# Weights times values of the prompt: three passes over halves in place of one full-precision product

## The chip, the cores and the metric

The kernel runs on one core of one Trainium2 chip. The metric is the device time in microseconds of one execution; the profile is of one execution and gives the start and the length of each instruction on TensorE (PE, with its weight loads as PEld), VectorE (DVE), ScalarE (ACT), GpSimd (POOL) and the DMA queue of SyncE (SP).

## What is computed

One step of a hybrid decoder layer: half a SwiGLU feed-forward, a mixer (differential attention beside a gated short convolution), half a second SwiGLU. 1040 prompt positions (16 meta tokens and 1024 real ones) and 64 sample positions (8 sequences of 8, each with 1024 cached positions) go through it. The change touches only the attention of the prompt:

```python
def diff_attend(q, k, v, q_pos, k_pos, lam):
    s = jnp.einsum('bqhcd,bkhcd->bhcqk', q.astype(jnp.float32), k.astype(jnp.float32)) * (HEAD_DIM ** -0.5)
    mask = k_pos[None, :] <= q_pos[:, None]
    s = jnp.where(mask, s, NEG_INF)
    p = jax.nn.softmax(s, axis=-1)
    a = p[:, :, 0] - lam * p[:, :, 1]
    return jnp.einsum('bhqk,bkhe->bqhe', a, v.astype(jnp.float32))
```

There are 4 heads, two softmax maps of 64 columns in each, and values of 128 columns. Everything is float32.

## The kernel before, in words

The program has three stages: the first feed-forward with the input projection, the attention (the stage of this change), and the output projection with the second feed-forward. In the first and the last, TensorE multiplies in three passes: each operand is split into a high half `hi` (ACT copies it, rounded to the type float32r) and a low half `lo` (DVE subtracts `hi` from the original), and the helper `three` (lines 168 to 171) issues high times high, high times low, low times high. Each of the three is one weight load and one product. A product of plain float32 operands stands in the trace as two weight loads and two products.

In the attention stage the prompt is done in 36 jobs: 4 heads times 9 blocks of queries, in the order 8, 6, 7, 4, 5, 2, 3, 0, 1 of `qi` (block 0 is the 16 meta tokens, block `qi` has 128 queries and sees `qi` blocks of 128 keys and a last one of 16). A job has three steps, and three jobs run staggered:

- `scores` (qk, line 929): scores of both maps, already in three passes; DVE takes them out of PSUM with mask and running maximum (line 939).
- `weights`: exponentials on ACT, then POOL and DVE form the difference of the two maps.
- `flip`: TensorE transposes the weights, up to four 128x128 blocks into the one PSUM bank `fl` (line 967); they are copied to SBUF into `at` by DVE or ACT in turn (lines 969 and 970); then, for each block of keys, a plain float32 product with the values adds to the bank `po` (line 982). Blocks are added up over `j`. Every second job ends with a norm over `po` (`sub_norm`, lines 901 to 906).

The values of a head come by DMA (`load_v`) into `vbuf`, two buffers deep. `at` is four buffers deep. Between the steps of the prompt stand the turns of the samples' attention (the bank `sa`, lines 1024, 1046, 1059, 1063, 1072), spread evenly over the jobs. A scheduler orders the instructions within each engine; each engine then works in that order. SP's queue issues the loads.

## Time and profile before

| what | us |
|---|---|
| median of 3 runs (2293.79 to 2299.85) | 2297.01 |
| time of the profiled execution | 2293.83 |
| span of its trace | 2292.1 |
| PE busy over the span | 2136.1 |
| DVE, ACT, POOL busy over the span | 1404.7, 929.5, 299.8 |

The span runs from the first to the last instruction; 1.7 us of the profiled time lie around it. Busy time of PE counts each product to the modelled end of its pipeline, so that products overlap; how fast PE goes is read from the distance between starts. [...]

### The profile page before, as it was taken

What the parts mean: (1) busy time and instruction counts of PE and PEld (TensorE: products, weight loads), DVE (VectorE), ACT (ScalarE), POOL (GpSimd) and SP (SyncE); (2) the same over time, 40 slices, a digit from 0 to 9 for tenths busy, and PEclk for the clock granted to TensorE, in tenths of its full rate; (3) what the DMA queues carried; (4) which work ended last, traced back from release to release, by engine and by line L of the source; (5) the groups of instructions that cost most, each with busy time, mean ns of one, the idle gap of its engine ahead of it and who ended that gap; (6) DMA issues with size and microseconds to landing.
All of it is one profiled execution on the core that took longest, in us unless ns stands there. A gap on an engine that the chain in (4) does not pass through costs nothing.

```text
span 2292.1 us, 41517 instructions
## 1 busy us (share of the span) xinstructions
PE 2136.1 (93%) x16126; PEld 2038.4 (89%) x16126; DVE 1404.7 (61%) x2973; ACT 929.5 (41%) x1960; POOL 299.8 (13%) x419
## 2 busy tenths in 40 slices
PE   6899999999999979999799978749999999999997
PEld 5799999999999959999667768739999999999997
DVE  5766556655567775466457656765665665645756
ACT  7433333334254442333235555553333333332522
POOL 0111111110000004443302110001111111100000
PEclk9899999999999989999789889879999999999998
DMA  7121222235444313321567332112122222543443
GB/s 276 55 81 67 81 81 68 81 116 197 130 144 142 131 51 120 124 86 60 191 206 274 125 137 102 67 35 78 67 81 81 68 80 81 175 144 127 141 148 98
DMA packets 115240, 263.48 MB, mean 115 GB/s; under 512 B 14514, under 2 KB 56114, under 8 KB 107602
## 3 DMA queue, kind: packets, MB, share of 16 engines
q1 hardware_dynamic: 109698, 244.92, 31.7%
q0 software_dynamic: 5344, 15.90, 1.9%
q8 instruction: 126, 2.06, 0.4%
q14 instruction: 72, 0.59, 0.1%
HBM read 206.47 MB, written 61.97 MB: 117 GB/s over the span
## 4 chain that ended last, share of the span: by engine, by line
PE 51%; issue 31%; DVE 7%; POOL 5%; DMA 3%; ACT 2%; SPq 1%; POOLq 0%; ACTq 0%; DVEq 0%
PE mm L169 13%; PE mm L170 13%; PE mm L171 13%; POOL u L440 3%; POOL n L440 3%; PE po L982 2%; PE mm L296 2%; PE qk L929 2%; DVE X L176 2%; PE fl L967 1%; PE sa L1059 1%; PE st L204 1%; PE sa L1024 1%; DVE Y L546 1%; DVE Y L543 1%
## 5 line engine op out<-in xcount | busy, mean ns | idle before, releaser
L169 PE MATMUL mm<-X,W 128*128 128x276 f32 x3868 | 1130.1, 292 | 27.8 <-ACT W L175 10.5
L170 PE MATMUL mm<-X,W 128*128 128x276 f32 x3868 | 1127.2, 291 | 2.8 <-DVE X L176 2.8
L171 PE MATMUL mm<-X,W 128*128 128x276 f32 x3868 | 1126.6, 291 | 1.9 <-DVE W L176 1.9
L169 PEld LDWEIGHTS mm<-X,W 128*128 128x128 f32 x3868 | 732.0, 189 | 31.0 <-ACT W L175 11.4
L170 PEld LDWEIGHTS mm<-X,W 128*128 128x128 f32 x3868 | 733.0, 190 | 4.3 <-DVE X L176 4.0
L171 PEld LDWEIGHTS mm<-X,W 128*128 128x128 f32 x3868 | 733.3, 190 | 3.2 <-DVE W L176 3.2
L176 DVE TENSOR_TENSOR W<-WR,W 128x512 fp32r<-128x512 f32 (+3 forms) x421 | 329.1, 793 | 116.4 <-ACT W L175 114.8
L175 ACT ACTIVATE W<-WR 128x512 fp32r<-128x512 f32 (+3 forms) x421 | 284.1, 689 | 249.6 <-PE mm L170 134.8
L420 ACT ACTIVATE n<-mm 128x276 f32<-128x276 f32 x210 | 84.2, 401 | 317.5 <-PE mm L171 299.0
L586 DVE TENSOR_TENSOR Y<-Y,mm 128x276 f32<-128x276 f32 x288 | 126.3, 439 | 128.1 <-PE mm L171 123.4
L440 POOL TENSOR_TENSOR u<-u,R 128x276 f32<-128x276 f32 x93 | 75.1, 807 | 493.2 <-ACT u L471 265.3
L440 POOL TENSOR_TENSOR n<-n,R 128x276 f32<-128x276 f32 x83 | 65.4, 787 | 547.2 <-ACT n L449 547.2
L170 PE MATMUL mm<-X 128*128 128x276 f32 x416 | 121.9, 293 | 2.7 <-DVE X L176 2.7
L169 PE MATMUL mm<-X 128*128 128x276 f32 x416 | 123.0, 296 | 1.5 <-ACT X L175 1.5
L423 DVE TENSOR_TENSOR n<-mm,n 128x276 f32<-128x276 f32 x105 | 46.8, 445 | 125.7 <-PE mm L171 113.9
L171 PE MATMUL mm<-X 128*128 128x276 f32 x416 | 121.4, 292 | 0.0
L221 ACT ACTIVATE sq<-Y 128x276 f32<-128x276 f32 x168 | 68.2, 428 | 86.4 <-DVE Y L586 58.7
L176 DVE TENSOR_TENSOR X<-X 128x552 fp32r<-128x552 f32 x104 | 75.5, 728 | 38.4 <-ACT X L175 37.9
L169 PE MATMUL mm<-X,X 128*128 128x276 f32 x320 | 93.9, 293 | 0.0
L170 PE MATMUL mm<-X,X 128*128 128x276 f32 x320 | 93.1, 291 | 0.0
L171 PE MATMUL mm<-X,X 128*128 128x276 f32 x320 | 93.1, 291 | 0.0
L929 PE MATMUL qk<-q,q 64*128 64x336 f32 (+10 forms) x360 | 69.9, 385 | 15.5 <-ACT q L175 11.1
(174 smaller groups left out, 2669.3 us busy)
## 6 DMA issues: line engine op xcount, KB each, us to landing
WR<-in_w_gu SPq DMA_DIRECT2D x43, 1024.0 KB, 4.8
WR<-in_w_dn SPq DMA_DIRECT2D x48, 640.0 KB, 3.9
X<-hid SPq DMA_DIRECT2D x88, 276.0 KB, 4.1
kp<-in_cache_k SPq DMA_DIRECT2D x64, 256.0 KB, 3.9
vp<-in_cache_v SPq DMA_DIRECT2D x64, 256.0 KB, 4.4
hid<-u SPq DMA_DIRECT2D x93, 138.0 KB, 1.8
hid<-n SPq DMA_DIRECT2D x83, 138.0 KB, 1.7
WR<-in_w_in SPq DMA_DIRECT2D x11, 1024.0 KB, 4.9
```

Source lines behind the costliest of these rows:

```text
L169: nc.tensor.matmul(ps, lh, rh, start=first, stop=False, **kw)
L170: nc.tensor.matmul(ps, lh, rl, start=False, stop=False, **kw)
L171: last_pe[0] = nc.tensor.matmul(ps, ll, rh, start=False, stop=last, **kw).ins
L175: tc.keep_in_program_order(act.activation(hi, raw, AF.Copy))
L176: on.tensor_tensor(lo, raw, f32(hi), op=ALU.subtract)
L221: act.activation(sq, src[:, s], AF.Square)
L296: last_pe[0] = nc.tensor.matmul(banks[n, g], w, lay["yv"][p][:, c, g * G:g * G + G], start=c == PAIR_K[0], stop=c == PAIR_K[-1]).ins
L420: act.activation(t, ps, AF.Copy)
L423: dve.tensor_tensor(self.n1, ps, self.n1, op=ALU.add)
L440: on.tensor_tensor(t, t, lay["R"][p][:, g * G:g * G + G], op=ALU.mult)
L586: dve.tensor_tensor(y, y, ps, op=ALU.add)
L929: last_pe[0] = nc.tensor.matmul(pw[m], a[r, q0:q0 + P], b[r, k0:k1], start=n == 0, stop=n == 2, tile_position=(m * DH, 0)).ins
```

## The change

The product of weights and values is made in three passes. The values get a second buffer for the high half, and a new function `split_v` splits them (for head 0 at the start of the stage, for each next head at the seventh job of the head before). `flip` no longer copies the transposed weights: for each piece of the bank `fl`, ACT copies the rounded high half out of PSUM, and then DVE subtracts it from the same piece of PSUM, which gives the low half. The four buffers of `at` become two pairs. The products go through `three`.

```diff
-    vs = ring("vs0", 1, 1152)
+    vs = ring("vs0", 1, 1152, F32R)
...
-    vbuf = [v.rearrange("p (j e) -> p j e", j=9) for v in vs + ring("vs1", 1, 1152)]
+    vbuf = [[v.rearrange("p (j e) -> p j e", j=9) for v in (lo, hi)]
+            for lo, hi in (vs + ring("vh0", 1, 1152, F32R), ring("vs1", 2, 1152, F32R))]
     pbuf = ring("p", 6, TP)
-    abuf = [a.rearrange("p (j q) -> p j q", j=9) for a in ring("at", 4, 1152)]
+    abuf = [[a.rearrange("p (j q) -> p j q", j=9) for a in ring(f"at{n}", 2, 1152, F32R)] for n in range(2)]
...
+    def split_v(h):
+        lo, hi = vbuf[h % 2]
+        halves(hi[:, 0:8, :], lo[:, 0:8, :], f32(lo[:, 0:8, :]), dve)
+        halves(hi[:N_META, 8, :], lo[:N_META, 8, :], f32(lo[:N_META, 8, :]), dve)
...
     for n in range(2):
         split_qk(0, n)
+    split_v(0)
...
-            at = of(abuf, "at")
+            lo, hi = of(abuf, "at")
...
-                copy = lambda dst, src: (dve.tensor_copy(dst, src) if (qi + j0 // 4) % 2
-                                         else act.activation(dst, src, AF.Copy))
                 n = len(js) - (js[-1] == qi)
+                parts = []
                 if n:
-                    copy(at[:, j0:j0 + n, :rows], ps[:, :n * P].rearrange("p (j q) -> p j q", q=P)[:, :, :rows])
+                    parts.append((ps[:, :n * P].rearrange("p (j q) -> p j q", q=P)[:, :, :rows], slice(0, P), slice(j0, j0 + n)))
                 if js[-1] == qi:
-                    copy(at[:N_META, qi, :rows], ps[:N_META, n * P:n * P + rows])
+                    parts.append((ps[:N_META, n * P:n * P + rows], slice(0, N_META), qi))
+                for src, r, j in parts:
+                    act.activation(hi[r, j, :rows], src, AF.Copy)
+                    dve.tensor_tensor(lo[r, j, :rows], src, f32(hi[r, j, :rows]), op=ALU.subtract)
...
             for j in range(qi + 1):
                 kr = N_META if j == qi else P
-                nc.tensor.matmul(po[:, off:off + rows], vt_[:kr, j, :], at[:kr, j, :rows], start=j == 0, stop=j == qi)
+                three(po[:, off:off + rows], vt_[1][:kr, j, :], vt_[0][:kr, j, :], hi[:kr, j, :rows], lo[:kr, j, :rows],
+                      j == 0, j == qi)
...
+            if step % 9 == 7:
+                split_v(nxt)
```

Ahead of the attention stage, and behind its last norm, each engine's order is unchanged. On TensorE, where head 0 flips its first job (block 8), before: `fl` are the transposes, `po` the products, `qk` scores of later jobs.

```order
L967 MATMUL fl_11659<-WR,p_11361 128x128 x4
L982 MATMUL po_11668<-at_11367,vs_777_11327 128x128 x4
L929 MATMUL qk_11873<-q_776_11326,q_775_11325 128x272
L929 MATMUL qk_11873<-q_774_11324,q_775_11325 128x272
L929 MATMUL qk_11873<-q_776_11326,q_773_11323 128x272
L929 MATMUL qk_12046<-q_776_11326,q_775_11325 128x320
```

The same place in the changed kernel; `at_820` holds high halves of the weights, `at_819` low ones, `vh_810` high halves of the values, `vs_777` low ones.

```order
L169 MATMUL po_11677<-at_820_11370,vh_810_11360 128x128
L975 MATMUL fl_11666<-WR,p_11363 128x128 x4
L170 MATMUL po_11677<-at_819_11369,vh_810_11360 128x128
L171 MATMUL po_11677<-at_820_11370,vs_777_11327 128x128
L169 MATMUL po_11677<-at_820_11370,vh_810_11360 128x128
L170 MATMUL po_11677<-at_819_11369,vh_810_11360 128x128
L171 MATMUL po_11677<-at_820_11370,vs_777_11327 128x128
L169 MATMUL po_11677<-at_820_11370,vh_810_11360 128x128
```

Four products have become twelve, and the second group of transposes now stands behind the first of the twelve. On DVE, at the start of the stage before, between the first score chunks of head 0 (`ISA` is the masked reduction of a chunk and the reading of its maximum):

```order
L939 ISA p_11362,mx_11588<-qk_11590,WR 128x336
L939 ISA mx_11588 128x1
L879 TENSOR_REDUCE ls<-t_11372 128x2
L939 ISA p_11361,mx_11588<-qk_11599,WR 128x352
L939 ISA mx_11588 128x1
```

And there in the changed kernel:

```order
L947 ISA p_11364,mx_11594<-qk_11596,WR 128x336
L947 ISA mx_11594 128x1
L887 TENSOR_REDUCE ls<-t_11374 128x2
L176 TENSOR_TENSOR vs_777_11327<-vs_777_11327,vh_810_11360 128x1024
L947 ISA p_11363,mx_11594<-qk_11605,WR 128x352
L947 ISA mx_11594 128x1
L176 TENSOR_TENSOR vs_777_11327<-vs_777_11327,vh_810_11360 16x128
```

The two subtractions of the first head's values stand between its score chunks. On DVE where the second job is flipped, before:

```order
L969 COPY at_11368<-fl_11838 128x256
L969 COPY at_11368<-fl_11838 16x128
L955 SCALAR_TENSOR_TENSOR p_11361<-p_11361,sm_12038,p_11362 128x528
L200 SCALAR_TENSOR_TENSOR t_11375<-po_11668,t_11375 128x128
L939 ISA p_11366,mx_12112<-qk_12114,WR 128x272
```

And in the changed kernel, where ACT has ahead of each of these subtractions a copy out of the same `fl`:

```order
L985 TENSOR_TENSOR at_821_11371<-fl_11859,at_822_11372 128x512
L963 SCALAR_TENSOR_TENSOR p_11363<-p_11363,sm_12101,p_11364 128x528
L947 ISA p_11368,mx_12187<-qk_12189,WR 128x272
L947 ISA mx_12187 128x1
L200 SCALAR_TENSOR_TENSOR t_11377<-po_11677,t_11377 128x128
```

A piece of 128x512, which only ACT handled in this job before, now passes through DVE as well.

## Rows read from the trace of the kernel before

**Rows 1.** The page: busy time of engines, and granted clock in 40 slices.

```profile
PE 2136.1 (93%) x16126; PEld 2038.4 (89%) x16126; DVE 1404.7 (61%) x2973; ACT 929.5 (41%) x1960; POOL 299.8 (13%) x419
...
PEclk9899999999999989999789889879999999999998
```

**Rows 2.** The chain of work from 1090 to 1380 us, shares by line.

```profile
by line: PE po L982 16.7%; PE qk L929 15.2%; PE fl L967 8.9%; PE sa L1059 7.2%; PE sa L1024 5.9%; PE mm L170 4.3%; PE mm L171 4.2%; PE mm L169 4.2%; SPq L992 3.7%; issue 3.1%; DMA q<-k_spill 3.1%; PE po L903 2.9%; PE sa L1046 2.7%; DMA kp<-
```

**Rows 3.** Stretches: from:to, length, busy us (instructions) by engine, PEclk, DMA share, GB/s.

```profile
1117.00:1347.00 230.00, 217.44 (x1782) 155.10 (x1782) 146.19 (x548) 111.39 (x291) 44.71 (x74) 0.89 0.55 183
...
1149.00:1160.00 11.00, 10.93 (x99) 7.82 (x99) 2.15 (x8) 0.64 (x2) 0.60 (x1) 0.54 0.73 226
1160.00:1167.00 7.00, 6.23 (x55) 5.05 (x48) 3.53 (x14) 4.98 (x9) 0.49 (x1) 0.99 0.63 190
1167.00:1174.00 7.00, 6.48 (x38) 2.44 (x38) 4.38 (x13) 3.03 (x11) 1.41 (x3) 0.52 0.16 46
1174.00:1259.00 85.00, 84.11 (x780) 58.60 (x778) 57.68 (x225) 44.70 (x116) 15.83 (x22) 1.00 0.77 261
1259.00:1262.00 3.00, 2.76 (x14) 2.54 (x14) 2.63 (x8) 0.95 (x4) 1.02 (x1) 0.50 0.68 251
1262.00:1303.00 41.00, 40.54 (x396) 29.56 (x395) 26.71 (x104) 21.57 (x59) 7.11 (x10) 0.99 0.43 138
1303.00:1314.00 11.00, 11.00 (x45) 5.95 (x44) 6.64 (x20) 6.38 (x14) 2.10 (x3) 0.53 0.33 110
1314.00:1320.00 6.00, 6.00 (x52) 5.20 (x49) 4.71 (x20) 2.77 (x8) 1.68 (x2) 1.00 0.01 3
1320.00:1324.00 4.00, 4.00 (x19) 3.00 (x18) 1.91 (x8) 2.03 (x7) 0.05 (x1) 0.57 0.00 0
```

**Rows 4.** PE's products of weights and values: ns min/median/max; eight at full, eight at half clock.

```profile
L982 PE MATMUL po<-at,vs x360: 257/275/579, 1137.1 to 1345.2; 128*128 128x128 f32 x144, 16*128 16x128 f32 x32, 16*128 16x16 f32 x4
...
1333.11 1.06 PE L982 MATMUL po<-at,vs 128*128 128x128 f32 x8
...
1260.15 1.91 PE L982 MATMUL po<-at,vs 128*128 128x128 f32 x8
```

**Rows 5.** Timeline, start and length in us: float32r loads, and plain products of 64 columns.

```profile
1335.36 0.41 PEld L929 LDWEIGHTS qk<-q,q 64*128 64x128 f32 x3 [0.17 <-DVE mx L939]
...
1202.38 2.14 PE L1046 MATMUL sa<-s_comb,s_p 128*128 128x64 f32 x18
```

**Rows 6.** Timeline of three passes with 276 columns, and their loads over the run (page).

```profile
1100.15 0.29 PE L171 MATMUL mm<-X,W 128*128 128x276 f32 x1
...
1100.27 0.29 PE L169 MATMUL mm<-X,W 128*128 128x276 f32 x1
...
1100.40 0.29 PE L170 MATMUL mm<-X,W 128*128 128x276 f32 x1
...
L169 PEld LDWEIGHTS mm<-X,W 128*128 128x128 f32 x3868 | 732.0, 189 | 31.0 <-ACT W L175 11.4
L170 PEld LDWEIGHTS mm<-X,W 128*128 128x128 f32 x3868 | 733.0, 190 | 4.3 <-DVE X L176 4.0
```

**Rows 7.** Lines, 1117 to 1347 us: count, busy us, mean ns, idle before and releasers.

```profile
L982 PE MATMUL po<-at,vs 128*128 128x128 f32 (+2 forms) x360 | 59.9, 298 | 1.1 <-DVE at L969 0.7 <-ACT at L970 0.4
L939 DVE CUSTOM_DVE_ANT_0 p<-qk,WR 128x336 f32<-128x336 f32 (+10 forms) x120 | 55.6, 480 | 41.4 <-PE fl L967 27.1 <-PE qk L929 13.6
...
L982 PEld LDWEIGHTS po<-at,vs 128*128 128x128 f32 (+1 forms) x360 | 48.6, 198 | 11.3 <-issue 3.7 <-DVE at L969 1.8 <-ACT at L970 0.7
...
L967 PE MATMUL fl<-WR,p 128*128 128x128 f32 (+2 forms) x180 | 34.2, 302 | 2.8 <-ACT at L970 1.9 <-DVE p L955 0.5 <-DVE at L969 0.3
...
L967 PEld LDWEIGHTS fl<-WR,p 128*128 128x128 f32 (+2 forms) x180 | 19.3, 140 | 13.6 <-ACT at L970 2.3 <-issue 2.2 <-DVE at L969 1.1
L969 DVE COPY at<-fl 16x128 f32<-16x128 f32 (+4 forms) x40 | 16.6, 439 | 4.9 <-PE fl L967 4.8
L970 ACT ACTIVATE at<-fl 16x128 f32<-16x128 f32 (+5 forms) x44 | 15.1, 371 | 30.8 <-PE fl L967 30.4
```

**Rows 8.** Lines by form: a split of 128x1024 elsewhere, on DVE and ACT.

```profile
L176 DVE TENSOR_TENSOR X<-WR,X 128x1024 fp32r<-128x1024 f32 x6 | 7.3, 1223 | 14.6 <-ACT X L175 14.6
...
L175 ACT ACTIVATE X<-WR 128x1024 fp32r<-128x1024 f32 x6 | 6.2, 1048 | 0.0
```

**Rows 9.** The start of the stage in the timeline: PE waits for DVE's score chunks.

```profile
1121.73 8.76 PE L929 MATMUL qk<-q,q 64*128 64x352 f32 x33 [1.65 <-DVE mx L939]
```

More of the change, by code (lines that the diff above doesn't have):

```diff
@@ L862, in load_v @@
     def load_v(h):
-        dma(vbuf[h % 2][:, 0:8, :], v_spill[h, :, 0:8, :])
-        dma(vbuf[h % 2][:N_META, 8, :], v_spill[h, :N_META, 8, :])
+        lo = f32(vbuf[h % 2][0])
+        dma(lo[:, 0:8, :], v_spill[h, :, 0:8, :])
+        dma(lo[:N_META, 8, :], v_spill[h, :N_META, 8, :])
+    def split_v(h):
+        lo, hi = vbuf[h % 2]
+        halves(hi[:, 0:8, :], lo[:, 0:8, :], f32(lo[:, 0:8, :]), dve)
+        halves(hi[:N_META, 8, :], lo[:N_META, 8, :], f32(lo[:N_META, 8, :]), dve)
     load_qk(0)
```

## The prediction

> **What bounds the kernel now.** I read the page first, then the chain of work around the attention, then that stage in stretches, then single rows of PE. PE is busy for 93% of the span, far ahead of DVE and ACT [rows 1]. The changed lines work from 1117 to 1347 us alone. There the chain runs mostly through PE: the products of weights and values (po) are its largest line, then the scores (qk) and the transposes (fl) [rows 2]. PE is busy for 217.4 of these 230 us, DVE for 146.2, ACT for 111.4 [rows 3]. So PE sets the pace, and only 12.6 us are free on it. The second thing to see is the clock: PEclk, close to 1 in the feed-forwards, dips in the slices of this stage [rows 1]. Cut by clock, the stage has 36 us at half clock between 1149 and 1324 (11, 7, 3, 11 and 4 us) [rows 3]. At full clock PE goes through 55 + 780 + 396 + 52 = 1283 instructions in 139 us, 9.2 in each us; at half clock through 99 + 38 + 14 + 45 + 19 = 215 in 36 us, 6.0 in each us, or 4.6 without the first stretch, which is full of small sample products. A us at half clock thus loses 1 - 6.0/9.2 = 0.35 to 1 - 4.6/9.2 = 0.50 us.
>
> **What one product costs.** There are 180 products of weights and values, which stand as 360 pairs of a weight load and a product [rows 4]. Eight of them take 1.06 us to the end of the last, whose own length is 0.275: their starts are (1.06 - 0.275)/7 = 0.112 us apart, so a plain product costs 2 x 0.112 = 0.224 us. At half clock eight take 1.91 us, about 0.22 apart. After the change the same product is three pairs. What does one pair with a 128-column stationary and 128 moving columns of float32r cost? No row has it, and two bounds stand around it. Below: the feed-forward's three passes start 0.125 us apart with 276 columns [rows 6], 0.45 ns a column, which for 128 columns would be 0.058 us if moving columns were all that counts. Above: the weight load. The loads of three float32r score products with only 144 columns start (0.41 - 0.19)/2 = 0.11 us apart (0.19 is the mean length of a load in [rows 6]). The plain products of line 1046 move half as many columns as those of line 982, and yet eighteen of them take 2.14 us, (2.14 - 0.275)/17 = 0.110 apart [rows 5]. Halving the columns saved nothing: with 128 stationary columns, the load sets the distance. I take 0.112 us. Nor is a load spared because the first two of the three passes share their stationary: the feed-forward has the same sharing, and both passes have 3868 loads [rows 6].
>
> [...]
>
> **The change, step by step.**
> 1. PE: 180 more pairs at 0.112 us are 20.2 us. At the present share of half clock, 36 of 175 us (20%), they cost a further 180 x 0.2 x (0.22 - 0.112) = 3.9 us. Sum 24 us. The 16-row blocks cost one more load like the others. PE is the busy engine and works in order, so I hide none of it; if all the idle 12.6 us took it up, 11 would stay.
> 2. ACT and DVE: 84 copies (40 on DVE, 44 on ACT, 31.7 us together [rows 7]) become 84 copies on ACT and, behind each, 84 subtractions on DVE. At the mean lengths of these rows that is 84 x 0.371 + 84 x 0.439 = 68 us: 16 us more on ACT, 20 more on DVE. Both stay under PE (127 and 166 of 230 us). What counts is that a group of transposes now passes two engines in a row before the bank `fl`, of which there is one, is free, and before the second of the three passes can start. Behind a waiting transpose on PE stand scores and sample products, and DVE in turn already waits 27.1 us for transposes at its score reductions [rows 7]. Before, PE stood idle for the copies for 1.9 + 0.3 + 0.7 + 0.4 = 3.3 us, and its loads for 5.9 us: 10 to 19% of the copies' 31.7 us. The same share of the added 36 us is 4 to 7 us; I take 5. Ends: 0, if the scheduler's other work between the groups covers it (the order shows scores put there), and all 36.
> 3. The values' split: 1.05 us on ACT and 1.22 on DVE [rows 8], and a small piece, four times. For head 0 it stands on DVE between the first score chunks, for which PE already waits 1.65 us [rows 9]; I add 1.5 us there. The other three lie in the middle of the stage under PE, at nothing: if that cover is gone, 4.5 us. The two new buffers only move addresses. `at` gets two buffers in place of four, which holds a flip back only if two jobs' products are outstanding; in the order a job's products stand close behind its flip. Nothing for that.
> 4. The clock. This is the term that no row prices. What PE did before its falls at 1259 and 1303 was scores, transposes and small sample products; plain po products belong to what it did in the long stretch at full clock. [...] I take the half clock to grow from 36 to about 100 us of a stage of some 270 us: 64 us more, at the middle price of 0.43, are 27.5 us. Ends: none more, 0; and all of the remaining full-clock work, 139 us plus the added 20, at half clock: 159 x (9.2/6.0 - 1) = 85 us.
>
> Sum: 24 + 5 + 1.5 + 27.5 = 58 us. The profiled execution took 2293.8 us, 3.2 under the median of the runs shown, so it would become 2351.8, and on the scale of the median 2355 us.
>
> **The rivals.**
> - *The clock holds* (slower, but by less). For it: PE will be as busy as before, and from 1174 to 1259 the clock stayed up through the same mixture. Against it: each fall came out of a mixture that was already near one. Steps 1 to 3 alone are 30 us: 2327 us; with the loads' part of step 2 covered, 2319.
> - *The clock stays down* for nearly all of the stage. [...] Against it: the sample products of line 1059 are spread over the whole stage, and after them the clock rose (1314). 30 + 85 = 115 us: 2412 us or over.
> - *Products cost what they stream* (faster). If a float32r load hides behind the product ahead of it better than these rows show, the pair costs the lower bound of 0.058 us: three are 0.174 against 0.224, 9 us less over 180 products. With 1.5 us for the split and the flips covered it ends at 2290 us; it decides from 0.072 us a pair, where the gain, 180 x (0.224 - 3 x 0.072) = 1.5 us, is no more than the split costs. [...] Against it stand the rows of lines 929 and 1046.
> - *The second load is spared.* The product then costs two loads, as now, and only steps 2 and 3 stay: 2297 to 2304 us. Against it: the equal counts of loads in the feed-forward.
>
> **How the numbers follow.** I give the forecast 0.55 (2333 to 2395), the clock that holds 0.26, the clock that stays down 0.12, products at the price of streaming 0.03, the spared load 0.04. What a measurement of this kernel can tell from no change is 0.3%, 6.9 us, so faster is under 2290 and slower over 2304. The streaming case lies on its lower edge and gives 0.02 to faster and 0.01 to no change; the spared load gives 0.03 to no change and 0.01 to slower; everything else is slower: 0.94. The range that leaves out 2 in 10 reaches from 2316, the low end of the holding clock, to 2400.
>
> **What would show it.** In the profile of the changed kernel: 540 products of weights and values with 540 loads, eight of them in a row at full clock still near 0.11 us apart (streaming case: near 0.06; spared load: a third fewer loads). The stage, 230 us before, at 255 to 265 (clock holds) or near 285, the rest of the span unchanged to a few us. Half-clock stretches that sum to some 100 us between the stage's first rise and its end. Idle of PE for the lines that split the weights under 15 us. I am wrong above all if the granted clock of the stage stays where it is, or if PE's waits for the splits, not its products, make up the growth.

## The result and the profile after

The changed kernel takes 2395.63 us (median of 4 runs, 2391.38 to 2403.27), the kernel before on the same chip 2295.40 (4 runs, 2288.08 to 2299.85). The ratio is 1.0444, interval [1.0402, 1.0485]: slower by some 100 us. The forecast was 2355, in a range of 2316 to 2400.

First the page of the changed kernel, the lines that answer to [rows 1].

```profile
PE 2224.4 (93%) x16306; PEld 2109.3 (88%) x16306; DVE 1430.6 (60%) x3025; ACT 949.1 (40%) x2008; POOL 296.5 (12%) x419
...
PEclk9899999999999989997778757888999999999998
```

There are 180 more instructions on PE and as many more loads, and ten slices in a row stand at 5 to 8 tenths of TensorE's full clock, where before the lowest was 7 and nines stood between. Next the stretches of the changed kernel, as in [rows 3]: from:to, length, then busy us (instructions) of PE, PEld, DVE, ACT and POOL, then PEclk (the share of the full clock that was granted, in the mean of the stretch), DMA share and GB/s. The first is the whole stage; the others are four stretches at one level of the clock each, and the two at its end. Behind the dots stands the last head of the kernel before.

```profile
1117.00:1455.00 338.00, 306.58 (x1967) 225.27 (x1967) 176.98 (x608) 138.56 (x348) 44.77 (x78) 0.70 0.41 133
1179.00:1200.00 21.00, 20.89 (x180) 14.64 (x173) 10.11 (x44) 8.87 (x28) 1.84 (x4) 0.99 0.65 207
1251.00:1275.00 24.00, 22.02 (x205) 17.05 (x202) 14.62 (x58) 12.35 (x35) 2.92 (x6) 0.99 0.67 225
1309.00:1336.00 27.00, 23.91 (x268) 16.45 (x267) 17.18 (x56) 13.54 (x34) 3.77 (x6) 1.00 0.50 164
1336.00:1360.00 24.00, 23.49 (x95) 16.57 (x95) 9.12 (x39) 7.70 (x24) 1.24 (x3) 0.50 0.06 16
1374.00:1439.00 65.00, 60.18 (x227) 49.33 (x226) 26.21 (x94) 24.05 (x69) 8.73 (x15) 0.50 0.03 11
1439.00:1462.00 23.00, 12.41 (x44) 10.00 (x44) 9.59 (x16) 9.57 (x19) 1.08 (x2) 0.50 0.68 253
...
1324.00:1348.00 24.00, 20.36 (x129) 15.29 (x127) 15.47 (x62) 14.21 (x45) 7.01 (x13) 0.99 0.13 42
```

The mean clock of the stage went from 0.89 [rows 3] to 0.70. At full clock PE still goes through (180 + 205 + 268)/72 = 9.1 instructions a us, at half clock through (95 + 227)/89 = 3.6 in these two stretches, the thinnest ones; over all stretches at half clock from 1152 to 1439 it is 778 in 163 us, 4.8. From 1374 on, through the rest of the last head, the clock does not come back at all. In the kernel before, the last head ran from 1324 to 1348 at 0.99.

From here on the stage is counted from its first score product to the first product of the output projection: 237.7 us before, 332.6 after. The rows of the stage counted so, before and after:

```profile
1117.30:1355.00 237.70, 217.42 (x1782) 155.08 (x1782) 148.10 (x553) 113.43 (x294) 45.50 (x76) 0.88 0.56 184
...
1119.50:1452.10 332.60, 304.56 (x1963) 224.11 (x1963) 173.09 (x605) 133.52 (x342) 42.79 (x76) 0.71 0.40 131
```

The rest of the span is 2054.3 and 2057.0 us, so 94.9 of the 97.5 us between the two traces lie in this stage. PE's idle time in it went from 20.3 to 28.0 us.

Now the products themselves, in the timeline of PE of the changed kernel: start, length, line. The first three and the 16-row pair stand at full clock, the last three at half.

```profile
1265.80 0.28 PE L169 MATMUL po<-at,vs 128*128 128x128 f32 x1
1265.91 0.27 PE L170 MATMUL po<-at,vs 128*128 128x128 f32 x1
1266.02 0.27 PE L171 MATMUL po<-at,vs 128*128 128x128 f32 x1
...
1267.40 0.27 PE L170 MATMUL po<-at,vs 16*128 16x128 f32 x1
1267.51 0.27 PE L171 MATMUL po<-at,vs 16*128 16x128 f32 x1
...
1425.09 0.41 PE L170 MATMUL po<-at,vs 128*128 128x128 f32 x1
1425.31 0.41 PE L171 MATMUL po<-at,vs 128*128 128x128 f32 x1
1425.52 0.41 PE L169 MATMUL po<-at,vs 128*128 128x128 f32 x1
```

The starts are 0.11 us apart at full clock and 0.215 at half, just as the plain pairs of [rows 4] were (0.112 and 0.22). The pairs of a block of 16 rows are as far apart as those of 128, 0.11 us, and their loads are as long: 249 ns in the mean against 252 in line 171. Three passes are thus 0.336 us where one plain product was 0.224.

Then the groups of the stage that answer to [rows 7]: busy us, mean ns, idle before and releasers.

```profile
L171 PE MATMUL po<-at,vs 128*128 128x128 f32 (+2 forms) x180 | 60.1, 334 | 0.0
...
L985 DVE TENSOR_TENSOR at<-fl,at 16x128 fp32r<-16x128 f32 (+5 forms) x84 | 35.8, 427 | 20.5 <-ACT at L984 20.0
...
L984 ACT ACTIVATE at<-fl 16x128 fp32r<-16x128 f32 (+5 forms) x84 | 32.2, 384 | 86.5 <-PE fl L975 69.4 <-DVE at L985 16.8
```

84 copies and 84 subtractions take 32.2 + 35.8 = 68.0 us, as forecast to the us. New are the two waits between them: DVE waits 20.0 us for ACT's high half, and ACT 16.8 us for DVE to give the bank `fl` free.

### The profile page after: what moved, and what is told of

It is laid out like the page before. It is cut to its first block, busy times and chain, and to the rows that moved or that the text cites. A ratio compares the mean times of both kernels' runs of the same rounds, so it can differ in the third digit from the quotient of the medians.

```text
span 2389.6 us, 41983 instructions
## 1 busy us (share of the span) xinstructions
PE 2224.4 (93%) x16306; PEld 2109.3 (88%) x16306; DVE 1430.6 (60%) x3025; ACT 949.1 (40%) x2008; POOL 296.5 (12%) x419
## 4 chain that ended last, share of the span: by engine, by line
PE 59%; issue 22%; DVE 8%; POOL 4%; DMA 4%; ACT 3%; SPq 1%; POOLq 0%; ACTq 0%; DVEq 0%
PE mm L169 16%; PE mm L170 16%; PE mm L171 16%; POOL u L440 2%; PE qk L937 2%; PE mm L296 2%; DVE X L176 2%; POOL n L440 2%; PE po L169 1%; PE po L170 1%; PE fl L975 1%; PE po L171 1%; PE sa L1070 1%; DMA hid<-u 1%; PE sa L1035 1%
## 5 line engine op out<-in xcount | busy, mean ns | idle before, releaser
L937 PE MATMUL qk<-q,q 64*128 64x272 f32 (+10 forms) x360 | 84.6, 423 | 18.1 <-ACT q L175 10.9
```

What stands on the lines that cost most here:

```text
L937: last_pe[0] = nc.tensor.matmul(pw[m], a[r, q0:q0 + P], b[r, k0:k1], start=n == 0, stop=n == 2, tile_position=(m * DH, 0)).ins
```

## The experiments

Every run is given as a ratio to the kernel before on its own chip (medians there 2293.45, 2295.17 and 2288.02 us for the three groups of runs). Of each profile I read the stage from first score to first product of the output projection, in a row of the same form as above. The half-clock time is the sum of the stretches of the stage whose granted clock is half; 2 x (1 - PEclk) x length gives it from the row to some 3 us.

**One part at a time.** Four kernels take the change apart. The first has the splits of the weights but no use for them: the product is the plain one, of the high half alone (the low half and the values' split leave the result).

```diff
-                three(po[:, off:off + rows], vt_[1][:kr, j, :], vt_[0][:kr, j, :], hi[:kr, j, :rows], lo[:kr, j, :rows],
-                      j == 0, j == qi)
+                nc.tensor.matmul(po[:, off:off + rows], f32(vt_[0][:kr, j, :]), f32(hi[:kr, j, :rows]), start=j == 0, stop=j == qi)
```

> The weights are split as in the changed kernel (84 copies on ACT, 84 subtractions on DVE out of the one bank), but the values are not, and the product is the plain one of before, of the high half alone, so the low half of the weights is left out of the result. TensorE's work is that of before, the chain behind each group of transposes that of the changed kernel. Theory (three loads per product and the half clock make the growth): 5 to 25 us over the kernel before, 2300 to 2320 us. Rival (the waits for the two-engine split make it): most of the 100 us, 2360 to 2395 us.

It took 2336.39 us, ratio 1.0180 [1.0150, 1.0211]: 43 us over, between the two forecasts and far more than the first. First its stage row, then its waits (us in all, times, the longest), then the wait for the score reductions in the kernel before.

```profile
1119.70:1400.20 280.50, 247.20 (x1782) 173.27 (x1782) 167.00 (x597) 128.66 (x334) 45.18 (x76) 0.81 0.48 156
```

```profile
PEld po L991 <- ACT at L983: 17.5, 26, 1.9
...
PEld qk L936 <- DVE mx L946: 16.4, 29, 2.2
...
PE po L991 <- ACT at L983: 10.4, 16, 1.7
...
PE qk L936 <- DVE mx L946: 7.4, 14, 1.8
```

```profile
PEld qk L929 <- DVE mx L939: 9.0, 16, 2.1
```

PE does the same 1782 instructions as before, though in another order (as in the change, a job's next transposes now stand behind products of its first group), and stands idle for 280.5 - 247.2 = 33.3 us (before 20.3). Loads wait 17.5 us for the high half, where they waited 0.7 for ACT's copy and 1.8 for DVE's [rows 7]. The other large wait is at the scores: loads wait 16.4 us for DVE's score reductions, 9.0 before. DVE, it seems, is held up at the subtraction and comes late to the next scores.

The clock fell here too: the half-clock time of the stage is 106 us against 57 before, with the same products. So the chain alone, without one pass more, brings 50 us more of half clock.

The second keeps three passes but has one copy for each piece, by ACT and DVE in turn as before; the low half is left out (the high half stands in for it).

```diff
-                    act.activation(hi[r, j, :rows], src, AF.Copy)
-                    dve.tensor_tensor(lo[r, j, :rows], src, f32(hi[r, j, :rows]), op=ALU.subtract)
+                    copy(hi[r, j, :rows], src)
...
-                three(po[:, off:off + rows], vt_[1][:kr, j, :], vt_[0][:kr, j, :], hi[:kr, j, :rows], lo[:kr, j, :rows],
+                three(po[:, off:off + rows], vt_[1][:kr, j, :], vt_[0][:kr, j, :], hi[:kr, j, :rows], hi[:kr, j, :rows],
```

> One copy out of the bank per piece, by ACT or DVE in turn as before, values split, three passes that all take the high half of the weights (the low half is left out of the result). TensorE's work is that of the changed kernel, the chain that of before. Theory: 60 to 90 us over the kernel before, 2355 to 2385 us, with the half clock filling most of the last head. Rival (waits): 0 to 25 us, 2295 to 2320 us.

2330.76 us, ratio 1.0144 [1.0098, 1.0190]: 37 us over, between the two forecasts. Its stage row:

```profile
1120.20:1399.50 279.30, 261.73 (x1962) 199.78 (x1962) 153.68 (x560) 117.83 (x302) 44.38 (x76) 0.77 0.47 157
```

The third has one copy and two passes (low and high half of the values times the high half of the weights): as many loads and products as the kernel before, 360, but of float32r.

```diff
...
+                for n, v in enumerate((vt_[1], vt_[0])):
+                    nc.tensor.matmul(po[:, off:off + rows], v[:kr, j, :], hi[:kr, j, :rows], start=j == 0 and n == 0,
+                                     stop=j == qi and n == 1)
```

> As the run with three passes and one copy, but only two passes: high and low half of the values times the high half of the weights. [...] Theory (the thinner products themselves take the clock down): 25 to 60 us over the kernel before, 2320 to 2355 us, with more half clock in the stage. Rival (only the number of loads counts, and the clock follows the waits): within 10 us of the kernel before, 2287 to 2305 us.

2312.52 us, ratio 1.0092 [1.0059, 1.0125]: 19 us over, again between the two forecasts. Its stage row, and three of its passes in a row:

```profile
1120.50:1375.70 255.20, 234.76 (x1783) 170.29 (x1783) 153.28 (x561) 118.08 (x302) 44.41 (x76) 0.78 0.51 172
...
1183.14 0.27 PE L994 MATMUL po<-at,vh 128*128 128x128 f32 x1
1183.25 0.27 PE L994 MATMUL po<-at,vs 128*128 128x128 f32 x1
1183.36 0.28 PE L994 MATMUL po<-at,vh 128*128 128x128 f32 x1
```

Same count of pairs, same copies, nearly the same order on PE, the same 0.11 us between starts, PE's idle time as before (20.4 us against 20.3), and yet the half-clock time is 112 us against 57. What differs for PE is the kind of product: a float32r pass of 128 columns behind each load, where the plain product was. The values' split is in this kernel too, so that 17.5 us of stage are the price of both. Between the second and the third lie 180 pairs: 24.1 us of stage, with 17 us more of half clock.

One thing more lies between them. The function `three` also marks its last product as the one behind which the next turn of the samples is queued on TensorE (lines 171 and 1109); the plain product did not. This is in the change and in every run that calls `three`, and no run takes it out alone.

The chain alone (the first kernel) lengthens the stage by 42.8 us and the passes with the values' split (the second) by 41.7, each with the half clock that it brings. Together that is 84.5 of the 94.9 us; by ratio it is 74 of 102, and the rest needs both at once, or is noise.

The fourth adds work to the changed kernel that nobody reads: after the last turn of the samples, one float32r product of 512 columns for each key block, into an unread bank.

```diff
+                if not turns:
+                    nc.tensor.matmul(bank("sa"), vt_[1][:, 0, :], kh[:, :512], start=True, stop=True)
```

> The changed kernel, and once the samples are done one product more per block of keys: float32r, 128 rows, 512 moving columns, into a bank that nobody reads; about 30 products of 0.23 us at full clock, 7 us of added work. Theory (the clock of the last head is lost for want of dense work): 10 to 35 us under the changed kernel, 2360 to 2385 us, with full clock back between the end of the samples and the end of the stage. Rival (loads and waits, the clock is only a symptom): 5 to 10 us over the changed kernel, 2400 to 2406 us.

2408.41 us, ratio 1.0500 [1.0468, 1.0533]. The forecast missed: the 29 products did not bring the clock back, which stood at half for 1380 to 1435 and 1441 to 1475 us. Wide passes of this kind and number did not do it here. Four of them in a row, at half clock:

```profile
1421.81 2.07 PE L993 MATMUL sa<-q,vs 128*128 128x512 f32 x4
```

The median length is 0.735 us, so they start (2.07 - 0.735)/3 = 0.44 us apart; at full clock that would be some 0.22, an estimate from the 0.11 and 0.215 us of the narrow passes above, near the 0.23 of the forecast (512 columns at the 0.45 ns of [rows 6], an estimate as well).

**The clock.** So another sort was tried: the same added product, but of plain float32.

```diff
+                if not turns:
+                    nc.tensor.matmul(bank("sa"), f32(vt_[1][:, 0, :]), f32(kh[:, :512]), start=True, stop=True)
```

> The changed kernel with work added that nobody reads: once the samples' work is used up, one plain float32 product of 512 columns per key block into an unread bank, some 29 of them, about 25 us at the full clock (0.85 each) and up to 50 at half. Theory A, the half clock of the last head comes from thin products that leave the array idle while weights load, and a product that is wide and goes through more than one pass brings the clock back: half-clock time in the last head falls from 89 us to under 40, and the time is within 10 us of the changed kernel (2385 to 2405). Theory B, the clock is set by something else there: the half-clock stretch stays, and the time is 30 to 50 us over the changed kernel (2425 to 2445).

2403.31 us, ratio 1.0480 [1.0457, 1.0504], 8 us over the changed kernel by ratio, with intervals that overlap, though the 29 products add about 25 us of work: they are 58 pairs with a median length of 0.593 us, and four of these in a row start (1.88 - 0.593)/3 = 0.43 us apart. These four, then the stretches from the last samples to the projection in this kernel:

```profile
1412.92 1.88 PE L993 MATMUL sa<-q,vs 128*128 128x512 f32 x4
1414.73 0.50 PE L937 MATMUL qk<-q,q 64*128 64x16 f32 x3
...
1377.00:1404.00 27.00, 27.00 (x77) 18.00 (x77) 9.20 (x28) 6.21 (x16) 4.20 (x7) 0.50 0.03 8
1404.00:1452.00 48.00, 46.40 (x220) 29.33 (x218) 18.73 (x67) 17.60 (x53) 4.41 (x9) 1.00 0.06 18
```

In the middle of the last head the clock comes back from 0.50 to 1.00 and stays for 48 us, where the changed kernel had half clock throughout. What the first theory forecast came: with other work beside the same passes the clock was back. The reason that it gives, what the array does while weights load, was not shown. Nor is it shown whether it was the kind of work or its amount: 58 pairs at 0.43 us are 25 us, 29 float32r passes at the estimated 0.22 us are 6, so that this run added four times the work of the one before.

The other question on the clock is whether PE's idle time sets it. In the kernel before, PE is busy for 0.2 of the 11 us before the first scores (1106 to 1117) and for 0.4 of the 9 us before the output projection (1346 to 1355), and the clock stands at 0.50 behind both (1117 to 1121, 1355 to 1362). So products of constants were put into these two gaps of the kernel before (helper `warm`, 45 and 38 plain products of 128 columns, unread).

```diff
+    def warm(tag, n, after):
+        ps = bank(tag)
+        with tc.issue_after(after):
+            for _ in range(n):
+                nc.tensor.matmul(ps[:, :P], onesD, onesD, start=True, stop=True)
...
+    warm("sa", 45, last_pe[0])
...
+    warm("st", 38, norm_pe[0])
```

> The kernel before, with products of constants that nobody reads put where PE idles ahead of a fall of the clock: 45 plain 128 by 128 products ahead of the first scores of the attention stage (PE idle there for 11 us, and half clock right behind it) and 38 ahead of the output projection (9 us idle). Theory A, the clock falls there for the idle time, and these products keep it up: the half-clock stretch at the start of the stage goes, and the time is 4 to 12 us under the kernel before (2281 to 2289). Theory B, the fall comes from the thin products that follow, or the added products delay the first scores by as much as they save: within 4 us, or up to 8 us over.

2295.02 us (12 runs), ratio 0.9998 [0.9982, 1.0015]: no change, as the second theory had it. Its stretches at the start of the stage:

```profile
1106.00:1122.00 16.00, 15.07 (x130) 14.88 (x128) 2.72 (x5) 1.98 (x2) 4.91 (x8) 1.00 0.57 184
1122.00:1138.00 16.00, 14.78 (x106) 11.16 (x110) 12.56 (x43) 5.24 (x11) 6.20 (x18) 0.57 0.61 187
```

The clock stands at 1.00 through the gap, and falls to 0.57 all the same with the first scores. The half clock of the stage is 31 us against 57 and the stage 6.9 us shorter, but the first scores start 4.9 us later and the part behind the stage is 4.4 us longer. So the half clock at these waits cost little here, and what took it away cost as much.

**The split chain.** If the waits are for DVE's subtraction, the products with the low half could go last in each job:

```diff
...
+            for a, vs_ in ((hi, (1, 0)), (lo, (1,))):
+                for j in range(qi + 1):
+                    kr = N_META if j == qi else P
+                    for v in vs_:
+                        last_pe[0] = nc.tensor.matmul(po[:, off:off + rows], vt_[v][:kr, j, :], a[:kr, j, :rows],
+                                                      start=a is hi and j == 0 and v == 1, stop=a is lo and j == qi).ins
```

> The changed kernel with the order of the products within a job turned round: for each piece of weights first the two products that take the high half (low values times high, high values times high) for all key blocks, and the products that take the low half at the end. The same 540 load and product pairs, the same splits. Theory A, the waits of the split chain are for VectorE's subtraction, the later of the two reads: PE's waits at the products on VectorE (5.6 us in the changed kernel) go, the bank of the transposes is still held as long, so 5 to 15 us under the changed kernel (2380 to 2391). Theory B, what costs is the hold of the one transpose bank and the clock, not which half is ready first: within 4 us of the changed kernel (2391 to 2400).

2426.61 us, ratio 1.0573 [1.0550, 1.0595]: 30 us over the changed kernel, outside both forecasts. Its stage row and its waits, and after them the wait for ACT of the changed kernel:

```profile
1118.90:1482.40 363.50, 339.71 (x1962) 250.30 (x1962) 175.71 (x604) 135.24 (x342) 44.19 (x76) 0.62 0.37 120
```

```profile
PEld po L994 <- ACT at L984: 15.6, 22, 1.3
...
PE po L994 <- ACT at L984: 8.2, 15, 0.9
```

```profile
PEld po L169 <- ACT at L984: 6.5, 11, 1.3
```

The wait for DVE is gone, as meant, but the loads now wait 15.6 us for ACT (6.5 in the changed kernel): with the low products away, PE seems to reach the second piece of a job sooner, when its high half is not there yet. And the half clock grew from 196 to 275 us. That this follows from the order of the same 540 pairs is shown; why the clock took it so badly is not.

The other way is to free the bank after one read: a raw copy out of PSUM as before, and the split from that copy in SBUF, high half by ACT, low half by POOL.

```diff
...
+                    copy(raw[r, j, :rows], src)
+                    act.activation(hi[r, j, :rows], raw[r, j, :rows], AF.Copy)
+                    gp.tensor_tensor(lo[r, j, :rows], raw[r, j, :rows], f32(hi[r, j, :rows]), op=ALU.subtract)
```

> The changed kernel with one copy out of PSUM for each piece, by ScalarE and VectorE in turn as in the kernel before, and the split made from that copy in SBUF: the high half by ScalarE, the low half by GpSimd. The transpose bank is free after one read again, and VectorE has 84 subtractions fewer and half of the copies. Theory A, the hold of the bank over two engines and VectorE's load (about 25 us by the runs with an unchanged product) are what the split chain costs: 10 to 30 us under the changed kernel (2365 to 2386). Theory B, it is the length of the chain up to the first product that costs: here it is longer by a third operation, so the same or up to 30 us over it (2395 to 2425).

2364.72 us, ratio 1.0299 [1.0277, 1.0322]: 33 us under the changed kernel by ratio. The stage row, then the groups of the split, and the difference of the two maps on DVE in this kernel and in the changed one:

```profile
1121.70:1424.60 302.90, 283.95 (x1962) 212.92 (x1962) 173.84 (x560) 147.79 (x386) 112.19 (x160) 0.74 0.44 144
```

```profile
L990 POOL TENSOR_TENSOR at<-ar,at 16x128 fp32r<-16x128 f32 (+5 forms) x84 | 66.6, 805 | 98.5 <-ACT at L989 76.2 <-PE sa L1062 8.1 <-issue 6.2
...
L977 PE MATMUL fl<-WR,p 128*128 128x128 f32 (+2 forms) x180 | 39.8, 340 | 0.6 <-ACT ar L986 0.6
...
L964 DVE SCALAR_TENSOR_TENSOR p<-p,sm,p 128x1040 f32<-128x1040 f32 (+8 forms) x36 | 40.3, 1121 | 6.6 <-POOL p L963 6.6
...
L963 DVE SCALAR_TENSOR_TENSOR p<-p,sm,p 128x1040 f32<-128x1040 f32 (+8 forms) x36 | 27.4, 761 | 12.3 <-POOL p L962 12.3
```

POOL's subtraction takes 805 ns in the mean, DVE's took 427, and the chain is an operation longer: had its length been the cost, this would have been slower. It is faster, and what the edit freed is the bank, after one read. DVE's part of the copies shrank, but its busy time in the stage did not (173.8 us against 173.1 in the changed kernel): while POOL was busy for 112 us in place of 43, DVE's 36 differences of the two maps, unchanged in form, took 1121 ns in the mean in place of 761. PE's idle time is 18.9 us, less than before the change.

**Fewer loads.** The last four do the products of two neighbouring query blocks together. In the second job of a pair, key blocks that both read in full are multiplied once with 256 columns of weights: 396 pairs in place of 540.

```diff
...
-    abuf = [[a.rearrange("p (j q) -> p j q", j=9) for a in ring(f"at{n}", 2, 1152, F32R)] for n in range(2)]
+    lo2, hi2 = [a.rearrange("p (j s q) -> p j s q", j=9, s=2) for a in ring("at", 2, 2304, F32R)]
...
+            wide = qi - 1 if qi in (3, 5, 7) else 0
+            for j in range(wide):
+                three(po[:, :2 * P], vt_[1][:, j, :], vt_[0][:, j, :], hi2[:, j], lo2[:, j], j == 0, False)
+            for q, o in ((qi - 1, 0), (qi, P)) if wide else () if qi in (2, 4, 6) else ((qi, off),):
+                for j in range(wide, q + 1):
...
```

> The changed kernel with the products of two neighbouring query blocks done together, in the second job of each pair: for the key blocks that both read in full, each of the three passes moves 256 columns of weights past one load of values. 396 load and product pairs in place of 540 (144 of them 256 columns wide), the same splits, the weights of a pair in one tile. Theory A, the half clock comes from passes so thin that the load of the values takes as long as the product: 144 pairs fewer are 14 us, half-clock time in the stage falls by 40 us or more from 196, some 15 to 20 us, and part of the chain's 25 us is covered because the first block of a pair is long ready: 30 to 60 us under the changed kernel (2335 to 2365). Theory B, the clock follows the waits and not the width: only the pairs are saved, 10 to 18 us under it (2377 to 2386).

2354.99 us, ratio 1.0294 [1.0271, 1.0318]: 34 us under the changed kernel by ratio. The stage row, one job's wide passes, and the group that waits:

```profile
1117.10:1412.40 295.30, 259.13 (x1819) 187.22 (x1819) 171.44 (x605) 133.63 (x342) 43.98 (x76) 0.75 0.45 148
```

```profile
1161.52 0.28 PE L171 MATMUL po<-at,vs 128*128 128x256 f32 x1
1161.65 0.28 PE L169 MATMUL po<-at,vh 128*128 128x256 f32 x1
1161.76 0.28 PE L170 MATMUL po<-at,vh 128*128 128x256 f32 x1
1161.88 0.28 PE L171 MATMUL po<-at,vs 128*128 128x256 f32 x1
```

```profile
L975 PE MATMUL fl<-WR,p 128*128 128x128 f32 (+2 forms) x180 | 40.1, 344 | 10.7 <-DVE at L985 10.1 <-DVE nm L955 0.3 <-DVE nm L1052 0.2
```

Passes of twice the columns start 0.12 us apart in place of 0.11: the second 128 columns cost 0.01 us. Half clock is 145 us, 51 less than in the changed kernel. PE's idle time however is 36.2 us: without products between, the transposes now run into the bank that DVE's subtraction still holds (10.1 us).

The same kernel with every product at 128 columns holds back the first block's products but saves no load. Against the paired kernel:

```diff
-            wide = qi - 1 if qi in (3, 5, 7) else 0
...
-            for q, o in ((qi - 1, 0), (qi, P)) if wide else () if qi in (2, 4, 6) else ((qi, off),):
-                for j in range(wide, q + 1):
...
+            for q, o in ((qi - 1, 0), (qi, P)) if qi in (3, 5, 7) else () if qi in (2, 4, 6) else ((qi, off),):
+                for j in range(q + 1):
...
```

> The kernel with paired products, but every product 128 columns wide: 540 pairs as in the changed kernel, those of the first query block of a pair held back to the job of the second. Only the cover of the split chain differs from the changed kernel. Theory A, the chain of ScalarE, VectorE and product is what PE waits for in the changed kernel: half of the jobs no longer wait, 8 to 20 us under it (2375 to 2388). Theory B, the held products are a longer run of thin passes, with more half clock: as the changed kernel or up to 20 us over it (2395 to 2415).

2380.76 us, ratio 1.0413 [1.0390, 1.0437]: some 7 us under the changed kernel, with an interval that overlaps its own. Half clock is 191 us, as there. So of the pairing's gain most comes with the width.

Both helps together, the split from SBUF and the paired products, with both diffs:

> Both changes that should help the changed kernel: one copy out of PSUM for each piece with the split made from it in SBUF by ScalarE and GpSimd, and the products of two neighbouring query blocks done together at 256 columns. Theory A, the gains add, since one frees the bank and VectorE and the other cuts pairs and half clock: 31 us of the first and 30 to 60 of the second, 60 to 90 under the changed kernel (2305 to 2335), still over the kernel before. Theory B, both cover the same wait: no more than 10 us under the better of the two (2330 to 2365).

2337.31 us, ratio 1.0212 [1.0196, 1.0227]. That is 53 us under the changed kernel by ratio, where the two gains add up to 67: they add for the most part. The time lies just over the first forecast and in the range of the second, but 18 us under the better of the two where the second allowed 10. It is still 49 us over the kernel before.

```profile
1117.90:1400.00 282.10, 261.57 (x1819) 190.05 (x1819) 172.05 (x561) 145.87 (x386) 113.08 (x160) 0.75 0.47 155
```

And the kernel before with its plain products paired, 264 pairs in place of 360:

```diff
...
+            wide = qi - 1 if qi in (3, 5, 7) else 0
+            for j in range(wide):
+                nc.tensor.matmul(po[:, :2 * P], vt_[:, j, :], at2[:, j], start=j == 0, stop=False)
...
```

> The kernel before with its plain products paired in the same way: 132 products in place of 180, 48 of them 256 columns wide, two load and product pairs for each, so 264 pairs in place of 360. Theory A, a plain product streams for as long as its load takes, so a wider one saves next to nothing of itself (48 times 0.02 us, 1 us) and the clock already holds; only the waits on the copies are covered better: within 4 us of the kernel before or up to 8 under it (2287 to 2299). Theory B, plain products too are bound by their loads: 96 pairs by 0.112, 11 us, and less half clock, 11 to 20 under it (2275 to 2284).

2293.66 us (12 runs), ratio 1.0025 [1.0012, 1.0038], against 2288.02: no gain, and if anything a loss of 6 us that its profile does not show (its stage is 2 us shorter; the profiled execution, 2286.27 us, was the fastest of the 12). Eight wide pairs at full clock, whose last takes 0.38 us:

```profile
1176.80 1.89 PE L985 MATMUL po<-at,vs 128*128 128x256 f32 x8
```

They start (1.89 - 0.38)/7 = 0.216 us apart, nearly as much as two pairs of 128 columns (2 x 0.112): a wide plain product of two pairs saves 2 x (0.224 - 0.216) = 0.016 us, about the 0.02 us of the first theory, where a float32r pass of twice the columns took 0.01 us more. No version found beats the kernel before.

**What the runs add up to.** With 0.112 us for each pair beyond 360 and 0.35 us for each us of half clock beyond 57 (the lower of the two prices that the forecast drew from [rows 3]), what is left of each stage is an estimate of what its split chain costs beside the clock. The runs with products added and those without a change to the split are left out.

| kernel | stage | over 237.7 | added pairs | half clock | its price | left |
|---|---|---|---|---|---|---|
| two passes, one copy | 255.2 | 17.5 | 0 | 111.8 | 19.3 | -1.8 |
| three passes, one copy | 279.4 | 41.7 | 20.2 | 129.2 | 25.3 | -3.8 |
| splits, plain product | 280.5 | 42.8 | 0 | 106.4 | 17.4 | 25.4 |
| the change | 332.6 | 94.9 | 20.2 | 196.1 | 48.8 | 25.9 |
| low half last | 363.5 | 125.8 | 20.2 | 274.8 | 76.3 | 29.3 |
| held, narrow | 321.0 | 83.3 | 20.2 | 191.2 | 47.0 | 16.1 |
| paired | 295.3 | 57.6 | 4.0 | 145.1 | 30.9 | 22.7 |
| split from SBUF | 302.9 | 65.2 | 20.2 | 156.1 | 34.8 | 10.2 |
| both | 282.1 | 44.4 | 4.0 | 142.2 | 29.9 | 10.5 |

One copy leaves nothing; the split out of the bank by two engines leaves 16 to 29 us; the split from SBUF leaves 10. The price of half clock is a fit, not a law: 0.35 was chosen, the first two rows by themselves would give about 0.3, and in the kernel with warm products 26 us less of it shortened the stage by only 6.9. With 0.50, the forecast's other price, the change would have 5 us left in place of 26, but the two rows with one copy -10 and -15. So the share of chain and clock inside the change depends on the price; that the chain alone costs 42.8 us of stage and the passes with the values' split 41.7 does not.

## Why the prediction was right in kind and short in size

1. *PE's pairs* (20.2 us, and 3.9 for the half clock of before): right. There are 540 loads and products at 0.11 us, and the two kernels with one copy lie 24.1 us apart over 180 pairs, the half-clock share included. With these distances the case in which products cost what they stream fell, and so did the spared load. The 16-row blocks cost what the others did (0.11 us a pair, above). That halving the columns saves nothing held for plain products between 64 and 128 columns (0.110 and 0.112 us a pair), not between 128 and 256 (0.216). Three passes took 0.336 us against 0.224 of the plain product.
2. *The split chain* (5 us): this step failed in size. I carried the copies' share of waits (10 to 19%) over to a chain of two engines; the operations took exactly the 68 us forecast, but the kernel with splits and a plain product, whose PE does the instructions of before, was 42.8 us longer in the stage: some 25 us beside its half clock, and 50 us more of half clock, which the step did not have at all. Its profile shows 13 us as idle time of PE, and loads that wait 15 us longer for the high half and 7 us longer for DVE's scores. In the changed kernel itself PE's own waits for the lines of the weights' split are some 9 us, under the 15 that the forecast named, so its loss does not show as such waits. The reason that the runs point to is the one bank `fl`, held by ACT and then DVE, with DVE's scores queued behind its subtraction: freeing the bank by one read took some 16 us of the 26 back, though the chain grew longer and DVE was as busy; putting the low half last did not help. How much of it is the bank, and how much the order on PE that the scheduler chose around it, no run separates. The two buffers of `at`, priced at nothing, held nothing back: ACT's copies waited for transposes and for DVE (69.4 + 16.8 of 86.5 us), for no product.
3. *The values' split* (1.5 us): too small to be seen by itself. The kernel with two passes carries it and has nothing left beside its half clock; the first scores start at 1119.5 us with it and at 1119.7 without (the plain product). No run takes it out alone.
4. *The clock* (64 us more of half clock at 0.43, 27.5 us): right as a cause, too small as a size. It was 139 us more (56.8 to 196.1, counted over the whole stage), at a lower price of about 0.35, so some 49 us. That it would grow to about 100 us was the author's estimate; no row or run gives that figure, and what the runs showed follows. The forecast's 36 us of before left out 15 us at the start of the stage and 7 at its end; by its own count, from the stage's first rise to its end, the changed kernel has 177 us in place of some 100. Two steps failed. One is that the fall was laid to the passes in place of the plain products alone: they bring 55 us (two passes, one copy) to 72 (three), but the splits with plain products bring 50 too. The other is the argument against a clock that stays down, that sample products are spread over the whole stage and the clock rose after them. The large ones (line 1070, line 1059 before) start their last at 1370 us. From there to the projection the changed kernel needs 82.4 us, 78.4 of them at half clock; the kernel before needed 43.4, with 12.7. In the runs with three passes and one copy this tail has 60 us at half clock, with two passes 23, with the plain product 13. So in this stage the passes of 128 columns bring more half clock, shown by the equal counts of the two-pass kernel (112 us against 57), and added work brought the clock back in the last head, shown by the plain products of 512 columns (0.50 to 1.00). Which property of the work counts is not settled: the wide float32r products, a quarter of that work, did not bring it back. The forecast's reading that no plain product of values stood before the falls was not exact either: four started at 1302.66, just ahead of the fall at 1303.

The sum with these sizes is 20 + 25 + 49 = 94 us for a stage that grew by 94.9. That it fits so well says little about the shares, since 0.35 was chosen; at 0.50 the same stage is 20 + 5 + 70. The errors of steps 2 and 4 went the same way, which put the forecast 40 us low and the time at the upper end of the range; the clock's own bound (85 us) and the chain's (36) held them. That the range held is in part luck: the median lies 4 us under its end, and one of the four runs, 2403.27 us, beyond it. In the forecast the low end of the holding clock stands as 2319 in one place and as 2316 in another, with no term for the difference; nothing here hangs on it.

## What to carry to other kernels

Before a plain product is taken apart into passes, count pairs of load and product: with 128 stationary and 128 moving columns each pair here took 0.11 us, float32r or plain, and three passes (0.336 us) were dearer than one plain product (0.224); widen the moving side first (0.12 us for a float32r pass of 256 columns). When a PSUM bank with a depth of one is read by two engines in a row, price the hold of the bank and the work queued behind the second engine, not the two operations, and reckon with half clock from the chain too (50 us here). Look for the part of a stage where the new work will stand alone, here the last head after the samples have ended: 39 of the 94.9 us were lost there.

## What was not expected of the hardware

- Equal counts of loads and products with equal distances at full clock (0.11 us) came with 112 us at half clock as float32r passes of 128 columns and with 57 us as plain products.
- The splits with the plain product of before, the same 1782 instructions on TensorE, had 106 us at half clock where the kernel before had 57.
- About 25 us of unread plain products in the last head cost 8 us by ratio, which the noise does not tell from nothing, and the clock came back from 0.50 to 1.00; 29 unread float32r products of the same width, some 6 us of work by estimate, did not bring it back, and cost 13 us by ratio.
- A float32r pass of 128 columns starts 0.11 us after the one before, one of 256 moving columns 0.12 us; a plain pair of 256 columns 0.216 us, about twice the 0.112 of one with 128.
- With GpSimd busy for 112 us of the stage in place of 43, VectorE's 36 differences of the two maps, unchanged in form, took 1121 ns in the mean in place of 761.
- With products in the gap ahead of the first scores the clock stood at 1.00 up to them, and fell with them nevertheless, to 0.57 over the next 16 us.
